# RoPE on 16 heads: the first tile's store cut into its first row and its other three rows

## The chip, the core and the metric

The kernel runs on one core of one Trainium2 chip. Its time is the device time of one execution in microseconds, as the median of several runs. One further execution was recorded by the hardware profiler; every duration of an instruction or a transfer below comes from that one.

## What is computed

Rotary position embedding with the heads split out. For x of 16 x 512 x 1024 floats, 16 heads of 64 numbers and tables cos and sin of 512 x 32:

```python
x = x.reshape(batch, seq, num_heads, head_dim)
x1, x2 = x[..., :half_dim], x[..., half_dim:]
rotated = concatenate([x1 * cos - x2 * sin, x1 * sin + x2 * cos], axis=-1)
```

So each number is read once and written once, 33.6 MB each way, with two products and one sum for each.

## The kernel before

**Tiles and rows.** Two batches form a group, so there are eight groups of 1024 positions. A group lies on 128 partitions with eight positions each; one position of every partition is a "row" here, 128 x 1024 floats or 4 KB per partition. There are 64 rows, u = 0 to 63. A tile is what one transfer moves: the first and the last group are cut into two tiles of four rows (2 MB), the six groups between are one tile of eight rows (4 MB). That makes ten tiles, 0 to 9, and rows 0 to 3 are tile 0.

**The ring.** `x_sb` holds 40 rows, five groups. Results are written over the input rows in it, so a load into the ring's second round (tiles 6 to 9) has to wait until the store of the group that lay there has landed.

**A row's work.** POOL multiplies the row, its halves swapped, by the signed sine table into `t2_sb` (line 252; mostly two rows at a time, eight rows of buffer). DVE multiplies the row by the cosine table into PSUM, `t1_ps` (line 286; three rows of buffer). Then either DVE adds the two back into the ring (line 297), or, for three rows in eight from row 4 to row 59, PE adds `t2_sb` to PSUM through an identity matrix (line 216) and ACT copies the result into the ring (line 183). For one row in eight of the large tiles DVE makes the sine product itself (line 279). All engines go through the rows in order, coupled by counting semaphores.

**Who issues transfers.** ACT issues the loads (`load`, line 152): tile 0, the two tables, then tiles 1 to 5 at the start. Each load of the second round stands in ACT's program behind the copy of a given row, and ACT first waits there until all stores of the old group have landed; `sem_out[k]` counts 16 for each store of group k, and `stores_of(k)` says how many there are. Copies of later rows are behind that wait. SP issues the stores (line 160): at the last row of each tile it waits until all sums up to that row are made (`wait_added`), and stores the tile. In the page and the views, q10 is ACT's queue of loads and q1 is SP's queue of stores; both are served by the same 16 DMA engines. A transfer reaches each DMA engine as eight packets, one for each of eight partitions: 16 KB each for a tile of four rows, 32 KB for one of eight.

Of the kernel before, what the change touches and what calls it, by code (L numbers as in the profile page):

```python
# [6 lines left out]
def bass_split_heads_rope_kernel(  # L7
# [20 lines left out]
    P = 128  # L28
    R1 = seq // P
# [11 lines left out]
    tiles = []  # L41
# [35 lines left out]
    with ExitStack() as stack:  # L77
        x_sb = stack.enter_context(nc.sbuf_tensor([P, RING, H, 2, HALF], fp32))
# [9 lines left out]
        sem_out = [stack.enter_context(nc.semaphore(f"out{k}")) for k in range(EARLY)]  # L88
# [20 lines left out]
        outr = out.rearrange("(c b) (s r) h d -> c (b s) r (h d)", b=2, r=R2)  # L109
        xs = x_sb[:].rearrange("p n h t d -> p n (h t d)")  # L110

        def in_dram(view, t):
            c, r0, n = tiles[t]
            return view[c][:, r0:r0 + n, :].rearrange("p r d -> p (r d)")

        def in_sbuf(t):
            c, r0, n = tiles[t]
            k = (c * R2 + r0) % RING
            return x_sb[:, k:k + n].rearrange("p n h t d -> p (n h t d)")

        def where(u):
            t, r = rows[u]
            return t, r, u % RING
# [7 lines left out]
        def wait_added(eng, u):  # L131

            if n_pe[u]:
                eng.wait_ge(sem_a, n_pe[u])
            if n_comb[u]:
                eng.wait_ge(sem_v, n_comb[u])
# [9 lines left out]

        def stores_of(k):

            return sum(c == k for c, _, _ in tiles)

        def load(eng, t):
            eng.dma_start(in_sbuf(t), in_dram(xr, t)).then_inc(sem_in[t], 16)  # L152
# [1 line left out]
        def on_sync(sp):  # L154
            for u in range(NU):
                t, r, k = where(u)
                if r == tiles[t][2] - 1:
                    wait_added(sp, u)
                    k = u // R2
                    sp.dma_start(in_dram(outr, t), in_sbuf(t)).then_inc(sem_out[k] if k < EARLY else sem_rest, 16)  # L160
            sp.wait_ge(sem_rest, 16 * sum(stores_of(k) for k in range(EARLY, NU // R2)))

        def on_scalar(ae):
            later = {}
            for t, (c, r0, n) in enumerate(tiles):
                if c * R2 + r0 + n <= RING:
                    load(ae, t)
                else:

                    later.setdefault((c * R2 + r0 - RING) // R2 * R2 + R2 - 1 + LAG, []).append(t)  # L170
                if t == 0:
                    for i, (table, sem) in enumerate(((cos, sem_cos), (sin, sem_sin))):
                        ae.dma_start(stage[:, i, :], table.rearrange("(s r) d -> s (r d)", r=R1)).then_inc(sem, 16)  # L173

            ae.wait_ge(sem_i, 2)
            ae.activation(pick[:], ident[:].rearrange("q (s h) -> q h s", h=2)[:, :, None, :].broadcast_to([P, 2, 2, P // 2]), COPY).then_inc(sem_g, 1)  # L176
            ae.wait_ge(sem_t, 2)
            ae.activation(s_sb[:, :, 0, :].rearrange("p (h r) d -> p h r d", h=2), tab_ps[:, :, 1], COPY, scale=-1.0)  # L178
            ae.activation(s_sb[:, :, 1, :].rearrange("p (h r) d -> p h r d", h=2), tab_ps[:, :, 1], COPY).then_inc(sem_s, 1)  # L179
            for u in range(NU):  # L180
                if PE2[u]:
                    ae.wait_ge(sem_e, n_pe[u])
                    ae.activation(xs[:, u % RING, :], t1_ps[:, u % NT1, :], COPY).then_inc(sem_a, 1)  # L183
                for t in later.get(u, ()):
                    k = tiles[t][0] - RING // R2
                    ae.wait_ge(sem_out[k], 16 * stores_of(k))
                    load(ae, t)
# [71 lines left out]
        def on_vector(ve):  # L259
# [44 lines left out]
            for u in range(NU + LEAD):  # L304
                if u < NU:
                    mul(u)
                if u >= LEAD and not PE2[u - LEAD]:
                    comb(u - LEAD)

        on_sync(nc.sync)  # L310
        on_scalar(nc.scalar)
        on_gpsimd(nc.gpsimd)
# [35 lines left out]
```

## Time and profile before

| | |
|---|---|
| median of 3 runs | 161.16 us (161.14 to 161.43) |
| the profiled execution | 161.35 us, span 159.9 us |
| busy: DVE, POOL, PE, ACT | 129.3, 131.8, 66.7, 23.7 us |
| DMA | 67.25 MB, mean 420 GB/s |
| stores: issue at (us) | 22.30, 33.67, 49.99, 65.83, 82.88, 102.95, 119.22, 135.56, 144.50, 150.83 |
| from issue to landing (us) | 19.3, 22.6, 25.6, 29.3, 29.8, 24.4, 21.3, 14.6, 10.6, 9.1 |
| second-round loads: issue at (us) | 56.31, 75.61, 95.16, 95.53 |
| from issue to landing (us) | 33.3, 33.4, 28.4, 42.6 |

The span runs from the first to the last instruction. In the page's row of slices each digit is the busy share of one fortieth of the span, in tenths. In the rows of the timeline the first number is the start, the second how long it lasted, then engine, line, operation and tiles; what stands in brackets is the idle time of that engine ahead of it and what ended it. ACTq and SPq are instructions that only issue a transfer. A DMA share over 1.00 comes from counting a packet whole in the stretch in which it starts.

### The profile page before, as it was taken

How to read it: one execution, taken by the hardware profiler on the slowest of the kernel's cores; microseconds unless marked ns; L12 is line 12 of the kernel's file. 1: busy time of each engine (PE TensorE's matmuls, PEld its weight loads, DVE VectorE, ACT ScalarE, POOL GpSimd, SP SyncE). 2: the span in 40 equal slices, each digit the busy share in tenths (PEclk: the TensorE clock that was granted, in tenths of full speed). 3: DMA queues.
4: the chain of work that ended last, by engine and by line, in shares of the span. 5: the costliest groups of instructions: out<-in, count | busy, mean ns of one | idle time of the engine just before them, and what ended most of it. 6: DMA issues, size and time to landing. Idle time of an engine off the chain costs nothing.

```text
span 159.9 us, 494 instructions
## 1 busy us (share of the span) xinstructions
PE 66.7 (42%) x94; PEld 22.6 (14%) x94; DVE 129.3 (81%) x115; ACT 23.7 (15%) x25; POOL 131.8 (82%) x41
## 2 busy tenths in 40 slices
PE   6050006338932762286209540098509860880000
PEld 1020002012301220122002110022102220220000
DVE  0009986799999999999799927999999989989700
ACT  0410000202220222020400204002500250031000
POOL 1009999999999999999999999599999999598000
PEclk9999999999995799569965998555985589567555
DMA  5999998999999999999999999999999999999896
GB/s 164 411 441 459 393 508 344 447 406 426 471 406 447 479 393 395 492 418 402 418 492 393 418 492 402 402 475 389 479 397 418 451 418 488 410 402 484 373 438 279
DMA packets 3169, 67.25 MB, mean 420 GB/s; under 512 B 352, under 2 KB 608, under 8 KB 608
## 3 DMA queue, kind: packets, MB, share of 16 engines
q10 hardware_dynamic: 1728, 33.69, 49.8%
q1 hardware_dynamic: 1440, 33.56, 48.7%
q14 instruction: 1, 0.01, 0.0%
HBM read 33.69 MB, written 33.55 MB: 420 GB/s over the span
## 4 chain that ended last, share of the span: by engine, by line
DMA 49%; DVE 16%; POOL 13%; issue 7%; PE 6%; ACT 2%; ACTq 1%; DVEq 0%; SPq 0%
DMA x_sb<-in_x_dram 27%; DMA out_dram<-x_sb 18%; POOL t_sb L252 13%; DVE x_sb L297 8%; DVE t_ps L286 6%; PE t_ps L216 5%; DMA stage<-in_sin_dram 4%; DVE t_sb L279 2%; ACT x_sb L183 1%; PE tab_ps L200 1%; ACTq L152 0%; ACTq L173 0%; ACT s_sb L178 0%; ACT s_sb L179 0%; DVE tab_ps L265 0%
## 5 line engine op out<-in xcount | busy, mean ns | idle before, releaser
L252 POOL TENSOR_TENSOR t_sb<-x_sb,s_sb 128x2048 f32<-128x2048 f32 (+1 forms) x35 | 131.1, 3775 | 14.9 <-ACT s_sb L179 10.3
L216 PE MATMUL t_ps<-t_sb,ident 128*128 128x512 f32 x84 | 61.9, 888 | 70.6 <-DVE t_ps L286 48.8
L286 DVE TENSOR_TENSOR t_ps<-x_sb,tab_ps 128x1024 f32<-128x1024 f32 x64 | 76.7, 1221 | 17.4 <-ACT s_sb L179 10.5
L297 DVE TENSOR_TENSOR x_sb<-t_ps,t_sb 128x1024 f32<-128x1024 f32 x43 | 52.3, 1219 | 3.2 <-POOL t_sb L252 3.1
L183 ACT ACTIVATE x_sb<-t_ps 128x1024 f32<-128x1024 f32 x21 | 21.3, 1024 | 111.6 <-PE t_ps L216 100.2
L216 PEld LDWEIGHTS t_ps<-t_sb,ident 128*128 128x128 f32 x84 | 20.7, 273 | 111.4 <-DVE t_ps L286 78.8
L279 DVE TENSOR_TENSOR t_sb<-x_sb,tab_ps 128x1024 f32<-128x1024 f32 x6 | 7.3, 1215 | 0.0
L200 PE MATMUL tab_ps<-stage,pick 128*128 128x256 f32 x4 | 2.0, 667 | 4.8 <-DMA stage<-in_sin_dram 4.8
L193 PE MATMUL t_ps<-zero 128*128 128x512 bf16 x6 | 2.7, 630 | 1.3 <-DVE zero L260 1.3
L200 PEld LDWEIGHTS tab_ps<-stage,pick 128*128 128x128 f32 x4 | 1.2, 324 | 5.9 <-issue 5.7
L176 ACT ACT_TABLE_LOAD x1 | 1.3, 1283 | 4.8 <-issue 4.8
L193 PEld LDWEIGHTS t_ps<-zero 128*128 128x128 bf16 x6 | 0.7, 138 | 2.3 <-DVE zero L260 1.2
L178 ACT ACTIVATE s_sb<-tab_ps 128x256 f32<-128x256 f32 x1 | 0.4, 384 | 4.4 <-PE tab_ps L200 4.4
L260 DVE MEMSET zero<- 128x256 uint32 x1 | 0.3, 272 | 0.9 <-PEq L330 0.9
L227 POOL MEMSET ident<- 128x128 f32 x1 | 0.2, 205 | 0.3 <-POOLq L330 0.3
L176 ACT ACTIVATE pick<-ident 128x256 f32<-128x256 f32 x1 | 0.4, 430 | 0.0
L179 ACT ACTIVATE s_sb<-tab_ps 128x256 f32<-128x256 f32 x1 | 0.4, 378 | 0.0
L229 POOL TENSOR_SCALAR_AFFINE_SELECT ident<-ident 128x128 f32<-128x128 f32 x1 | 0.3, 294 | 0.1
L330 POOL MEMSET const-float32-0.0<- 128x1 f32 x1 | 0.1, 99 | 0.3 <-issue 0.3
L265 DVE TENSOR_SCALAR tab_ps<-tab_ps 128x32 f32<-128x32 f32 x1 | 0.2, 189 | 0.0
L330 POOL MEMSET const-bfloat16-1.0<- 128x1 bf16 x1 | 0.1, 102 | 0.0
L330 POOL MEMSET const-uint8-127<- 128x1 uint8 x1 | 0.1, 102 | 0.0
(1 smaller groups left out, 0.1 us busy)
## 6 DMA issues: line engine op xcount, KB each, us to landing
x_sb<-in_x_dram ACTq DMA_DIRECT2D x6, 4096.0 KB, 33.5
out_dram<-x_sb SPq DMA_DIRECT2D x6, 4096.0 KB, 25.0
x_sb<-in_x_dram ACTq DMA_DIRECT2D x4, 2048.0 KB, 19.9
out_dram<-x_sb SPq DMA_DIRECT2D x4, 2048.0 KB, 14.9
stage<-in_cos_dram ACTq DMA_DIRECT2D x1, 64.0 KB, 7.3
stage<-in_sin_dram ACTq DMA_DIRECT2D x1, 64.0 KB, 7.0
```

Of the source, the lines that this page charges most:

```text
L176: ae.activation(pick[:], ident[:].rearrange("q (s h) -> q h s", h=2)[:, :, None, :].broadcast_to([P, 2, 2, P // 2]), COPY).then_inc(sem_g, 1)
L178: ae.activation(s_sb[:, :, 0, :].rearrange("p (h r) d -> p h r d", h=2), tab_ps[:, :, 1], COPY, scale=-1.0)
L179: ae.activation(s_sb[:, :, 1, :].rearrange("p (h r) d -> p h r d", h=2), tab_ps[:, :, 1], COPY).then_inc(sem_s, 1)
L183: ae.activation(xs[:, u % RING, :], t1_ps[:, u % NT1, :], COPY).then_inc(sem_a, 1)
L193: pe.matmul(t1_ps[:, k, b * BANK:(b + 1) * BANK], zero[:, 0:P], zero[:], start=True, stop=True).then_inc(sem_w, 1)
L200: pe.matmul(tab_ps[:, h].rearrange("p c r d -> p (c r d)"), pick[:, h].rearrange("q b s -> q (b s)"), stage[:].rearrange("q c f -> q (c f) ...
L216: ins = pe.matmul(t1_ps[:, u % NT1, b * BANK:(b + 1) * BANK], ident[:], t2[:, b * BANK:(b + 1) * BANK], start=False, stop=True, skip_group ...
L252: pl.tensor_tensor(t2_sb[:, u % NT2:u % NT2 + n], x_sb[:, k:k + n, :, ::-1, :], table[:, :, None, :, :].broadcast_to([P, n, H, 2, HALF]), ...
L279: ve.tensor_tensor(t2_sb[:, u % NT2, :, :, :], swapped(k), over_heads(tab_ps[:, 0, 1, V_ROW - 1:V_ROW + 1, :]), mult)
L286: ve.tensor_tensor(t1_ps[:, u % NT1, :].rearrange("p (h d) -> p h d", d=HALF), x_sb[:, k, :, :, :].rearrange("p h t d -> p (h t) d"), tab_ ...
L297: ve.tensor_tensor(xs[:, k, :], t1_ps[:, u % NT1, :], t2_sb[:, u % NT2, :, :, :].rearrange("p h t d -> p (h t d)"), add,).then_inc(sem_v, 1)
L330: nc = _bacc.Bacc("TRN2", target_bir_lowering=False, num_devices=1)
```

## The change

SP stores tile 0 in two transfers. As soon as row 0 is added it issues the store of that row alone, 128 x 4 KB; after row 3, where the whole tile was stored, it issues rows 1 to 3, 128 x 12 KB. Both count on `sem_out[0]`, which therefore gets three increments of 16 for group 0 where it got two. The other nine tiles are stored as they were.

```diff
         def stores_of(k):
-            return sum(c == k for c, _, _ in tiles)
+            return sum(c == k for c, _, _ in tiles) + (k == 0)
+
+        def rows_dram(p0, p1, r0, r1):
+            return outr[0][p0:p1, r0:r1, :].rearrange("p r d -> p (r d)")
+
+        def rows_sbuf(p0, p1, r0, r1):
+            return x_sb[p0:p1, r0:r1].rearrange("p n h t d -> p (n h t d)")
...
         def on_sync(sp):
             for u in range(NU):
                 t, r, k = where(u)
-                if r == tiles[t][2] - 1:
+                if u == 0:
+                    wait_added(sp, u)
+                    sp.dma_start(rows_dram(0, P, 0, 1), rows_sbuf(0, P, 0, 1)).then_inc(sem_out[0], 16)
+                elif u == R1 - 1:
+                    wait_added(sp, u)
+                    sp.dma_start(rows_dram(0, P, 1, R1), rows_sbuf(0, P, 1, R1)).then_inc(sem_out[0], 16)
+                elif r == tiles[t][2] - 1:
```

## The prediction

> **What bounds the kernel now.** I read the page's slices and queues first, then the stretches of the DMA queues, then the order of time around the waits. The page:
>
> ```profile
> DMA  5999998999999999999999999999999999999896
> ...
> DMA packets 3169, 67.25 MB, mean 420 GB/s; under 512 B 352, under 2 KB 608, under 8 KB 608
> ...
> q10 hardware_dynamic: 1728, 33.69, 49.8%
> q1 hardware_dynamic: 1440, 33.56, 48.7%
> ```
>
> The 16 DMA engines are busy from slice 2 to slice 38 of 40. Queue q10 (loads, issued by ACT) and q1 (stores, issued by SP) take 49.8 + 48.7 = 98.5% of the span, 157.6 of 159.9 us. The rest is the start (no packet before 1.8 us) and the end of the last store. The view of stretches agrees; its columns end with the granted clock, DMA share and GB/s:
>
> ```profile
> 56.00:138.00 82.00, 39.24 (x58) 13.25 (x57) 76.00 (x68) 14.12 (x14) 77.59 (x20) 0.76 1.00 429
> 138.00:150.00 12.00, 5.41 (x7) 1.53 (x6) 11.52 (x11) 2.05 (x2) 9.15 (x3) 0.64 0.99 429
> 150.00:154.00 4.00, 0.00 (x0) 0.00 (x0) 0.76 (x1) 0.00 (x0) 0.00 (x0) 0.50 1.02 438
> ```
>
> DMA is the bound. DVE and POOL (the third and fifth figures) are close behind and finish at 150.8, just ahead of the last stores. So the question is not whether a store can start earlier, but whether the same bytes cost more, and whether the DMA engines run dry anywhere.
>
> How the two queues share an engine, from the DMA view of four stretches (150 to 153, 57 to 67, 27 to 35 us); columns are packets, MB, share of 16 engines:
>
> ```profile
> q1 hardware_dynamic: 79, 1.29, 100.6%
> ```
> ```profile
> q10 hardware_dynamic: 70, 2.29, 53.1%
> q1 hardware_dynamic: 67, 2.20, 51.0%
> ```
> ```profile
> q10 hardware_dynamic: 71, 2.33, 70.8%
> q1 hardware_dynamic: 64, 1.05, 30.6%
> ```
>
> A 16 KB packet takes 1.006 x 3 x 16 / 79 = 0.611 us, a 32 KB load packet 0.531 x 10 x 16 / 70 = 1.214 us. So a packet costs (1.214 - 0.611) / 16 = 0.0377 us per KB and 0.008 us fixed. In the third stretch tile 0's 16 KB stores lie beside 32 KB loads: the counts are nearly equal (71 and 64), the time is not (70.8 and 30.6%). The queues take turns packet by packet, and the queue with small packets gets the smaller share.
>
> **The change part by part.** Nothing moves on DVE, POOL, PE or ACT; SP issues 11 stores for 10. The sum is made against the profiled execution, 161.35 us (its span 159.9 and 1.45 around it), 0.19 above the median 161.16.
>
> *Cost of the bytes.* Each DMA engine had eight 16 KB packets for tile 0 and gets eight of 4 KB (0.008 + 0.151 = 0.159) and eight of 12 KB (0.460): 8 x (0.159 + 0.460 - 0.611) = 0.06 us. Each transfer also leaves one small packet per engine (352 under 512 B are 22 transfers x 16); one more costs the fixed 0.008. Together **+0.07 us**. The extra SP issue (0.33 us) lies in SP's idle time: SP waited 21.5 us for the fourth sum.
>
> *When tile 0 and what follows is stored.* The first sum ends at 14.12 + 1.23 = 15.35, and SP issues 0.03 later, as it does for the fourth (22.27, issue at 22.30). That issue's first packet came 3.9 us on (none up to 26.2, 11 by 27.0), so row 0 starts at 19.3. Before: eight turns of 1.214 + 0.611, and one in which the store only closes: 15.8 us from 26.2 is 42.0; less 1.2 for the turn that a load gives up as tile 3's load closes in that time: 40.8 (on record 22.30 + 19.3 = 41.6). After: row 0, 8 x (1.214 + 0.159) + 1.2 = 12.2; rows 1 to 3, 8 x (1.214 + 0.460) + 1.2 = 14.6; 19.3 + 26.8 = 46.1, less 2.4 for two loads that close (tiles 2 and 3): 43.7. Tile 0 starts 6.9 us earlier and lands **2.9 us later**, since 17 turns beside big loads replace 8. If all of row 0 went in one turn, it would be done before 26.2 and tile 0 land 8 x 0.151 = 1.2 us earlier; equal counts in 2-us stretches (16 and 16 at 59 to 61) speak for turns of one packet. I take +2.9.
>
> *Who waits for that.* Tiles 1, 2 and 3 were issued (33.67, 49.99, 65.83) before the store ahead had landed, so they land 2.9 later too, at some 59, 78 and 98 us. ACT waits for these landings before it issues loads into the ring, and its PSUM copies are queued behind:
>
> ```profile
> 75.61 0.33 ACTq L152 DMA_DIRECT2D x_sb<-in_x_dram  x1
> 76.00 1.94 ACT L183 ACTIVATE x_sb<-t_ps 128x1024 f32<-128x1024 f32 x2 [4.21 <-DMA out_dram<-x_sb]
> ```
> ```profile
> 95.16 0.86 ACTq L152 DMA_DIRECT2D x_sb<-in_x_dram  x2
> 96.06 1.94 ACT L183 ACTIVATE x_sb<-t_ps 128x1024 f32<-128x1024 f32 x2 [7.23 <-DMA out_dram<-x_sb]
> ```
> ```profile
> 97.12 2.36 DVE L286 TENSOR_TENSOR t_ps<-x_sb,tab_ps 128x1024 f32<-128x1024 f32 x2 [4.14 <-ACT x_sb L183]
> ```
>
> DVE lost 1.12 us at 77.05 and 4.14 at 97.12 to this. With landings 2.9 later it resumes at 80.0 and 100.0: 2.9 in all, as the first delay moves the second wait's start along. From 97.2 to 150.8 DVE is busy 52.33 of 53.60, so at most 1.3 is made up. The last store is issued at 150.83 + 1.6 to 2.9 = 152.4 to 153.7.
>
> *Whether that reaches the end.* The store ahead of it lands at 144.50 + 10.6 = 155.1, and the last one at 150.83 + 9.1 = 159.9; its own data take 8 x 0.611 = 4.9, so landing follows the data by 0.3 to 0.4, and its first packet went at 154.7. With no load beside it an issue needs 1.0 us to its first packet (the kernel's first: 0.80 to 1.8); beside loads 3.9. The tail has no loads: 1.0. So 153.4 to 154.7 meets 154.7: cover is used up, nothing is lost. The store issued at 135.56 becomes 138.5 and needs its turn when the one ahead ends, at 119.22 + 21.3 - 0.4 = 140.1: enough. Loads, served more while stores have small packets, land 2 to 3 us earlier, which removes POOL's wait for the last load (1.94 at 138.16). Loads not yet due: tile 2 lands at 23.3, in the row's first turns some 0.5 later, and POOL needs it at 29.9.
>
> Sum: 161.35 + 0.07 = 161.42; on the median **161.25** (161.16 + 0.07, rounded up).
>
> A rule of the Trainium skill speaks against the change: "DMA: Bandwidth & Descriptors", section "Rules for kernel authors", wants at least 1 MiB per transfer for full bandwidth, and the page's anatomy section gives some 2.0 us fixed per DMA; the row's 0.5 MiB would by that, as an estimate, add up to 2 us if nothing covered it. Here a store follows a store with the DMA share at 1.02 (150 to 154 us), so the trace shows no such gap between queued transfers.
>
> **The rivals.** (1) *Later landings reach the end, slower.* One mechanism: tile 0's small packets, ACT's ring wait, DVE, last store. It decides once the last store's first packet comes after 154.7. With landings 4.1 later (no turn saved by loads that close) and nothing made up, the issue is at 154.9, the packet at 155.9: +1.2; with 3.9 us to the first packet and the 2.9 above, 152.4 + 3.9 = 156.3 to 157.6: +1.6 to +2.9. I price it at +0.8, 162.0, from 161.6 to 163. For it: DVE has no slack after 97. Against: no loads at the end. (2) *Stretched loads, slower.* Beside tile 0's store a load packet took 0.708 x 8 x 16 / 71 = 1.276 us and not 1.214. Some 8 load packets per engine lay there, 8 x 0.062 = 0.5 us; now 16 do: +0.5, 161.7. Against: nothing shows that it depends on the store. (3) *Faster.* The reverse of that stretch, or landings 1.2 earlier. Earlier landings alone shorten DVE's waits but not the DMA work, so they give nothing; a stretch that is gone gives -0.5, 160.75. (4) *A transfer's fixed time stands open* once: +2, 163.2; the gapless stores speak against it. That the change fails to start row 0 early is out: SP had nothing else to wait for.
>
> **How the numbers follow.** Forecast, DMA bound and cover just enough: 0.47 (161.0 to 161.5). Rival 1: 0.24. Rival 2: 0.09. Rival 3: 0.18. Rival 4: 0.02. A measurement tells about 0.2% from no change, 0.32 us. Faster 0.18, within 0.47, slower 0.35. The range 160.8 to 162.3 leaves out the upper part of rival 1, rival 4 and the lower half of rival 3, some 0.18.
>
> **What would show it.** Right: tile 0's two stores land near 31 to 32 and 44 us; ACT's load issues come near 59, 78.5 and 98; DVE's two waits grow to nearly 3 us more in all; POOL's wait on the last load is gone; DMA share stays at 1.0 up to 158. Wrong: those landings come no later (turns are not by packet), load packets beside tile 0 differ from 1.276, or a gap of DMA share before the last store.

## The result and the profile after

| | before | changed |
|---|---|---|
| median | 161.24 us (18 runs, 161.14 to 161.97) | 161.85 us (18 runs, 161.32 to 162.35) |
| profiled execution | 161.35, span 159.9 | 162.29, span 160.9 |
| last store: issue, from issue to landing | 150.83, 9.1 | 151.70, 9.1 |

The changed kernel takes 1.0029 times as long (95% interval 1.0016 to 1.0042): slower by 0.6 us at the median, a little over the 0.2% that the prediction took as not told from no change. Its runs also spread wide: the fastest (161.32) is next to the median of before, the slowest 1.1 us above it.

The page of the changed kernel, the lines that answer to those of before:

```profile
DMA  5999999999999999999999999999999999999994
...
DMA packets 3314, 67.25 MB, mean 418 GB/s; under 512 B 369, under 2 KB 625, under 8 KB 753
...
q10 hardware_dynamic: 1728, 33.69, 49.4%
q1 hardware_dynamic: 1584, 33.56, 48.5%
```

The shares give 97.9% of 160.9 = 157.5 us of DMA work for the mean DMA engine; before it was 98.5% of 159.9 = 157.5. **The mean work has not changed.** What has changed is how evenly the 16 DMA engines end. Every transfer leaves one packet under 512 B on each DMA engine as it closes (23 transfers x 16 are 368 of the 369 above), so the DMA view of short stretches counts closings. Near the end, in the stretches 158.4 to 159, 159 to 159.6 and from 159.6 on, before:

```profile
DMA packets 16, 0.05 MB, mean 82 GB/s; under 512 B 13, under 2 KB 13, under 8 KB 13
```
```profile
DMA packets 3, 0.00 MB, mean 0 GB/s; under 512 B 3, under 2 KB 3, under 8 KB 3
```
```profile
DMA packets 0, 0.00 MB, mean 0 GB/s; under 512 B 0, under 2 KB 0, under 8 KB 0
```

and in the changed kernel:

```profile
DMA packets 16, 0.03 MB, mean 55 GB/s; under 512 B 14, under 2 KB 14, under 8 KB 14
```
```profile
DMA packets 2, 0.02 MB, mean 27 GB/s; under 512 B 1, under 2 KB 1, under 8 KB 1
```
```profile
DMA packets 2, 0.02 MB, mean 5 GB/s; under 512 B 1, under 2 KB 1, under 8 KB 1
```

Before, 13 of 16 are done by 159 us and the last by 159.6. After, 14 are done by 159, and one DMA engine still has data to move after 159.6; it closes some 0.35 us before the landing at 151.70 + 9.1 = 160.8. That one sets the time. In all 14 profiled executions of this study the time is the close of the last DMA engine plus 1.76 to 1.92 us: before, it closes at 159.58 and the time is 161.35; after, 160.52 and 162.29. The other 15 close at much the same times in both, from 158.56 to 159.23 before and from 158.48 to 159.26 after.

The chain of waits by engine points elsewhere. Before, then after:

```profile
DMA 49%; DVE 16%; POOL 13%; issue 7%; PE 6%; ACT 2%; ACTq 1%; DVEq 0%; SPq 0%
```
```profile
DVE 35%; DMA 24%; issue 13%; PE 9%; POOL 9%; ACT 3%; ACTq 1%; DVEq 0%; SPq 0%
```

By that the kernel has turned from DMA bound to DVE bound, and the waits that feed this chain did grow. The changed kernel's timeline:

```profile
77.82 1.94 ACT L195 ACTIVATE x_sb<-t_ps 128x1024 f32<-128x1024 f32 x2 [6.20 <-DMA out_dram<-x_sb]
```
```profile
78.88 1.23 DVE L298 TENSOR_TENSOR t_ps<-x_sb,tab_ps 128x1024 f32<-128x1024 f32 x1 [3.11 <-ACT x_sb L195]
```
```profile
98.77 2.36 DVE L298 TENSOR_TENSOR t_ps<-x_sb,tab_ps 128x1024 f32<-128x1024 f32 x2 [3.97 <-ACT x_sb L195]
```

DVE resumes at 78.88 and 98.77 where it was 77.05 and 97.12. So two theories stood against each other:

- **Theory T, the tail:** later landings delay ACT and DVE, and the last store comes too late (the prediction's rival 1).
- **Theory S, the slowest DMA engine:** the chain of stores has cover, and the kernel ends when the slowest of 16 DMA engines has done its share; the change makes that one later.

### The profile page after: what moved, and what is told of

Its sections match the earlier page's. It is cut to its first block, busy times and chain, and to the rows that moved or that the text cites. A ratio compares the mean times of both kernels' runs of the same rounds, so it can differ in the third digit from the quotient of the medians.

```text
span 160.9 us, 495 instructions
## 1 busy us (share of the span) xinstructions
PE 65.7 (41%) x94; PEld 22.5 (14%) x94; DVE 129.2 (80%) x115; ACT 23.7 (15%) x25; POOL 131.7 (82%) x41
## 3 DMA queue, kind: packets, MB, share of 16 engines
q10 hardware_dynamic: 1728, 33.69, 49.4%
## 4 chain that ended last, share of the span: by engine, by line
DVE 35%; DMA 24%; issue 13%; PE 9%; POOL 9%; ACT 3%; ACTq 1%; DVEq 0%; SPq 0%
DMA out_dram<-x_sb 19%; DVE x_sb L309 16%; DVE t_ps L298 16%; POOL t_sb L264 9%; PE t_ps L228 8%; DMA stage<-in_sin_dram 4%; DVE t_sb L291 3%; ACT x_sb L195 3%; PE tab_ps L212 1%; ACTq L158 1%; ACTq L185 0%; ACT s_sb L190 0%; ACT s_sb L191 0%; DVE tab_ps L277 0%; DVEq L308 0%
## 5 line engine op out<-in xcount | busy, mean ns | idle before, releaser
L228 PE MATMUL t_ps<-t_sb,ident 128*128 128x512 f32 x84 | 60.9, 874 | 71.6 <-DVE t_ps L298 57.0
## 6 DMA issues: line engine op xcount, KB each, us to landing
out_dram<-x_sb SPq DMA_DIRECT2D x1, 1536.0 KB, 20.8
```

The costliest lines, as they stand in the source:

```text
L228: ins = pe.matmul(t1_ps[:, u % NT1, b * BANK:(b + 1) * BANK], ident[:], t2[:, b * BANK:(b + 1) * BANK], start=False, stop=True, skip_group ...
```

## The experiments

Each was timed beside the kernel before on the same chip; ratios are to it, with 95% intervals.

**1. The changed kernel again**, for a second trace.

> The changed kernel once more, for a second trace. Theory S (one straggling DMA engine): the mean DMA engine closes the last store at 158.8 us of the span as before, but one of the 16 closes 1 to 2 us behind the rest and sets the end; time 161.6 to 162.1. Theory T (the tail: tile 0's store lands later, ACT's wait for it delays DVE, and the last store comes too late): most DMA engines show a gap ahead of the last store and all close some 0.5 us later than before; time 161.6 to 162.1.

Measured: 161.80 us, 1.0026 (1.0013 to 1.0040). The profiled execution of this run took 161.31 us, as little as the kernel before, with its last store issued at 152.75, 1.05 us *later* than in the trace that took 162.29. Its closings in the three stretches are 10, 6 and 0; the last two of these:

```profile
DMA packets 6, 0.00 MB, mean 0 GB/s; under 512 B 6, under 2 KB 6, under 8 KB 6
```
```profile
DMA packets 0, 0.00 MB, mean 0 GB/s; under 512 B 0, under 2 KB 0, under 8 KB 0
```

The same program, a later last store and a faster run: against T. That the slowest DMA engine closes 1 us earlier (159.54 for 160.52), and so nearer to the rest, is S.

**2 and 3. ACT's waits taken off the copies**, in the changed kernel and in the one before:

```diff
-    LAG = 10
+    LAG = 14
```

> The changed kernel with ACT's second-round loads placed four rows later in its program (LAG 14 for 10), so that ACT no longer waits for landings ahead of its copies, and DVE's waits of 3.1 and 4.0 us go. The last store is then issued at some 147 to 149 us, not 151.7. Theory T: the cost of the change is gone, 161.2 to 161.35 us. Theory S: the last store's issue does not matter, 161.6 to 162.0 us.

> The kernel before with LAG 14. DVE's waits of 1.1 and 4.1 us go, the last store is issued at 147 to 148 us. Both theories have the DMA engines busy to the end, so 161.15 to 161.35, as before. Were it faster by over 0.3 us, the kernel before would have been bound by the tail, which neither theory says.

Measured: the changed kernel with it 161.59 us, 1.0020 (1.0002 to 1.0037); the kernel before with it 161.44, 1.0012 (1.0003 to 1.0021). Waits and SP's last issue in the former:

```profile
DVE t_ps L298 <- ACT x_sb L195: 0.8, 2, 0.4
```
```profile
147.34 0.33 SPq L172 DMA_DIRECT2D out_dram<-x_sb  x1
```

DVE's waits for ACT fell from 7.9 us to 0.8 and the last store is issued 4.4 us earlier, yet most of the cost may still be there; its runs reach from 161.21 to 162.36, as wide as the changed kernel's. T's forecast failed. The median lies at the lower edge of S's, and the intervals of 1 and 2 overlap, so whether a small part went is not told. The kernel before got slower by 0.1% from losing its DVE waits (1.6 us left of 6.9), which neither theory said.

**4. The split without the early start:** both transfers after row 3.

```diff
-                if u == 0:
-                    wait_added(sp, u)
-                    sp.dma_start(rows_dram(0, P, 0, 1), ...)
+                if u == 0:
+                    continue
                 elif u == R1 - 1:
                     wait_added(sp, u)
+                    sp.dma_start(rows_dram(0, P, 0, 1), ...)
                     sp.dma_start(rows_dram(0, P, 1, R1), ...)
```

> The two transfers, both issued after row 3: the split without the early start. Tile 0's turns start at 26.2, not 18.6, so tile 0 lands 6.5 to 7.5 us later than in the changed kernel (49 to 50 us), tile 1 at 63 to 65, and ACT's first wait for landings lasts until then. Theory T: DVE loses 6 to 8 us more, the last store is issued at 156 to 159 us, and the time is 164 to 167 us. Theory S: the same chain, but it costs only what passes the cover of 2 to 3 us: 162.5 to 165 us. If the time stayed at 161.9, the landings would not matter at all.

Measured: 162.15 us, 1.0052 (1.0036 to 1.0068), less than either theory gave. ACT's first load of the second round went at 62.85 (57.41 in the changed kernel), its third at 99.04 (96.78): of 5.4 us of delay 2.3 are left. While the load queue is dry, the stores have the DMA engines to themselves and catch up. The last store is issued at 154.63, and here the tail does show: all 16 DMA engines close late, between 160.38 and 160.55. DMA share (last figure but one) in 154 to 156 us:

```profile
154.00:156.00 2.00, 0.00 (x0) 0.00 (x0) 0.56 (x1) 0.00 (x0) 0.00 (x0) 0.50 0.71 303
```

**5. Each row of tile 0 alone.** SP issues a store after each of rows 0 to 3, four transfers of 4 KB packets.

```diff
-                if u == 0:
+                if u < R1:
                     wait_added(sp, u)
-                    sp.dma_start(rows_dram(0, P, 0, 1), ...)
+                    sp.dma_start(rows_dram(0, P, u, u + 1), ...)
```

> Each row of tile 0 stored alone as it is added: four transfers of 4 KB packets. 36 turns for 18 in the changed kernel, so tile 0 lands some 15 us later (57 to 60 us) and group 0 at 71 to 75; ACT waits for it from 58 on, the load queue runs dry for some 5 to 10 us, in which the store queue has the DMA engines alone. Both theories: DVE loses 10 us or more, the last store is issued past 160 us, and the time is 168 to 175 us. If turns are not by packet, the landing hardly moves and the time stays below 162.5.

Measured: 161.65 us, 1.0020 (1.0009 to 1.0030): far off my forecast. Group 0 landed at 33.43 + 29.6 = 63.0, not 71 to 75, for the reason of experiment 4: the loads ran dry after 57 us, and tile 1's store then met no load packets. The last store was issued at 153.56 and landed 6.3 us later, with no store left ahead of it. In this execution, which took 161.31 us, all 16 DMA engines closed between 159 and 159.6:

```profile
DMA packets 16, 0.00 MB, mean 0 GB/s; under 512 B 16, under 2 KB 16, under 8 KB 16
```

This gives the tail's bound: issue plus 6.3. A tail that ends at 159.9, as the kernel before did, may have its last issue at 153.6. The changed kernel's 151.70 left 1.9 us of cover.

**6. Three rows, then one.**

```diff
-                if u == 0:
-                    sp.dma_start(rows_dram(0, P, 0, 1), ...)
+                if u == R1 - 2:
+                    sp.dma_start(rows_dram(0, P, 0, R1 - 1), ...)
                 elif u == R1 - 1:
-                    sp.dma_start(rows_dram(0, P, 1, R1), ...)
+                    sp.dma_start(rows_dram(0, P, R1 - 1, R1), ...)
```

> Rows 0 to 2 stored after row 2, row 3 after row 3: the same two sizes as in the changed kernel in the other order, started 2.3 us before the kernel before and 4.6 us after the changed one. By turns tile 0 lands 4 to 5 us later than in the changed kernel (46 to 47 us), group 0 at 60 to 62. Theory T: last store issued at 153 to 155 us, time 162.2 to 164. Theory S: cover of 2 to 3 us holds for most of it, 161.6 to 162.6.

Measured: 161.46 us, 1.0016 (0.9993 to 1.0038), not told from no change, and below both forecasts. Its profiled execution was the slowest of the study but one, 163.19 us, with the last store issued at 153.35. In the stretches 159 to 159.6 and from 159.6 on:

```profile
DMA packets 16, 0.02 MB, mean 27 GB/s; under 512 B 15, under 2 KB 15, under 8 KB 15
```
```profile
DMA packets 3, 0.03 MB, mean 10 GB/s; under 512 B 1, under 2 KB 1, under 8 KB 1
```

Fifteen DMA engines are done where a fast run ends; one is 2 us behind. That is S; by T all 16 would be late.

**7. Two halves by partitions**, both after row 3, with 16 KB packets as before.

```diff
+                if u == R1 - 1:
+                    sp.dma_start(rows_dram(0, P // 2, 0, R1), ...)
+                    sp.dma_start(rows_dram(P // 2, P, 0, R1), ...)
```

> Tile 0 stored after row 3 in two transfers of 64 partitions each, 16 KB packets as before: one transfer more, no small packets, no early start. Tile 0 lands one turn (1.2 us) later than in the kernel before, much as in the changed kernel. Theory S (the slowest of 16 DMA engines ends the kernel; the change makes that one later): if one more transfer is what does it, 161.6 to 161.9 us; if the small packets or the early start do, 161.2 to 161.35. Theory T (late tail): as the changed kernel, 161.7 to 161.9.

Measured: 161.56 us, 1.0013 (1.0001 to 1.0024): between the forecast for "one more transfer does it" and the one for "it does not", so it settles neither.

**8 and 9. As many transfers as before, and one fewer.** Row 0 early and rows 1 to 7 in one transfer; then rows 0 to 7 in one.

```diff
+                elif u == R2 - 1:
+                    sp.dma_start(rows_dram(0, P, 1, R2), ...)    # in 9: 0, R2, and no row 0 ahead
```

> Row 0 stored early as in the changed kernel, then rows 1 to 7 in one transfer after row 7: as many transfers as the kernel before (10), with the early 4 KB packets. Group 0 lands at about 57 us (37.5 us to the first packet, then 8 turns of 1.214 + 1.06 and one that closes), so the chain through ACT and DVE is as in the changed kernel. If the eleventh transfer is what costs, the time is 161.2 to 161.35 us; if the early small packets cost, 161.6 to 161.9. Late tail: not decided by it, the last store still has some 1 us of cover.

> Group 0 stored once, rows 0 to 7 after row 7: nine transfers, no small packets, and the first store 11 us later than before. Group 0 lands at 56 to 58 us. If each transfer costs by itself, 160.9 to 161.2 us, under the kernel before; if the slowest DMA engine's one fetch of instructions sets the floor, 161.2 to 161.4. Only a dry DMA queue could make it slower, and the loads alone fill the DMA engines until 37 us.

Measured: 161.44 us, 1.0010 (0.9997 to 1.0024), and 161.44, 1.0010 (0.9997 to 1.0022). Neither is told from no change. The first median lies between the values that I had set for "the eleventh transfer" and "the small packets"; the second lies above both of its forecasts. So they settle nothing, but for one thing: a gain per transfer saved is not there.

**10 and 11. Load one DMA engine, change nothing else.** The kernel before with waits on SP that are already met; they become 128 and 320 instructions ahead of the first store (the pages count 622 and 814 for 494). SP is through with them in time: its first store goes at 22.26 and 22.15, for 22.30.

```diff
         def on_sync(sp):
+            for _ in range(256):      # 640 in 11
+                sp.wait_ge(sem_z, 1)
```

> The kernel before with 256 waits that are already met ahead of SP's first store: SP is idle then, so only its instructions have to be fetched (some 16 KB more, by the DMA engines). Theory S: the fetches take turns on one DMA engine and delay it by some 0.66 us each (in the kernel before a fetch record of 309 ns is followed by a store packet 350 ns longer than the others), so the slowest engine ends 0.6 to 1.3 us later if it is that engine: 161.8 to 162.6. Theory T: nothing waits for SP, so the time is 161.2 to 161.35 us.

> The kernel before with 640 idle waits on SP (320 instructions, some 19 us, done before the first store at 22.3), for 256 (128 instructions), which added one fetch record and 0.44 us. Slowest DMA engine: two or three fetches, 0.4 us each on the same DMA engine, 162.0 to 162.6 us, and the last DMA engine closes 1.3 to 1.9 us behind the mean. If the fetches spread over DMA engines: 161.8 again. If fetches were not the cause: 161.3.

Measured: 161.79 us, 1.0026 (1.0014 to 1.0038), its fastest run at 161.53, at the lower edge of S's forecast; and 163.69, 1.0145 (1.0126 to 1.0165), above the highest forecast, 162.6. Queue q14, which fetches instructions, in the kernel before, in 10 and in 11:

```profile
q14 instruction: 1, 0.01, 0.0%
```
```profile
q14 instruction: 2, 0.02, 0.0%
```
```profile
q14 instruction: 4, 0.03, 0.0%
```

The kernel before has one fetch in its span, at 63.1 us: one record of 0.31 us on one DMA engine, and the store packet behind it takes 1.57 us for 1.214, together 0.66 us. (The changed kernel also has one, at 60.6; its page counts a second record on q14, of 40 bytes.) One more raised the time by 0.44 us (161.79 less 161.35 beside it), three more by 2.4 (163.69 less 161.32). A load of 8 KB on one of 16 DMA engines, in 67 MB, costs nearly as much as the change: this shows S for the kernel before. In 11 the stretches 159 to 159.6 and from 159.6 on show it:

```profile
DMA packets 16, 0.02 MB, mean 27 GB/s; under 512 B 15, under 2 KB 15, under 8 KB 15
```
```profile
DMA packets 4, 0.05 MB, mean 14 GB/s; under 512 B 1, under 2 KB 1, under 8 KB 1
```

Fifteen DMA engines close by 159.35, one at 161.98. That one also delivers the last load late (POOL waits 6.0 us for loads, 1.9 before), which takes the tail along: the last issue is at 153.37.

Which DMA engine a packet ran on is not recorded, but it can be worked out. Without a gap, a packet's record starts 3 or 4 ns before the end of the one ahead of it on its DMA engine (all 1761 steps after 60 us in the changed kernel can be put so), and every DMA engine gets the same packets of each transfer; so the records fall into 16 lanes, one for each DMA engine. In the kernel before the lane with the fetch closes last, at 159.58. The added fetch does not join it. In 10 it comes at 9.8 us and its lane closes last, at 159.97; the fetch at 60.5 lies in another lane, which closes at 159.34. So a fetch counts only as far as its DMA engine ends behind the others, and 0.66 us on another one cost 0.44. In 11 at least two of the three added fetches lie in the lane that closes at 161.98; the fetch at 60.6 lies in one that closes at 159.35.

**12. Both at once:** the 256 waits in the changed kernel.

> The changed kernel with the same 256 idle waits on SP that added 0.44 us to the kernel before. They add one fetch of instructions to the DMA engine that fetches already. If the changed kernel's loss sits on that same DMA engine, the two add up: 162.1 to 162.4 us, and one DMA engine closes some 1.0 to 2.2 us behind the mean of 158.9. If its loss sits on other DMA engines or in the chain of stores, the later of the two counts alone: 161.75 to 161.95 us.

Measured: 161.64 us, 1.0019 (1.0002 to 1.0037): below both forecasts, of which the interval reaches only the one for the later of the two alone. The two do not add up, and the forecast for "the same DMA engine" rested on a premise that does not hold in the profiled execution: the two fetches lie in two lanes. The lane of the added fetch (9.6 us) closes at 159.67. The lane of the other (60.7 us) closes last, at 159.94, and has a store packet of 1.60 us at 126.2 besides.

## Why the prediction was right or wrong

The time fell into the range, but the likeliest case did not come true: 161.25 was forecast within 0.2%, 161.85 came, slower. That the range held is luck: rivals 1 and 2, priced at 162.0 and 161.7, had stretched it upward, and the time came out near their prices by neither's mechanism.

- **Cost of the bytes: right.** The DMA view of the changed kernel in 20 to 28 us, where row 0 is stored beside loads:

```profile
q10 hardware_dynamic: 112, 3.15, 91.1%
q1 hardware_dynamic: 111, 0.45, 13.8%
```

  A 4 KB packet takes 0.138 x 8 x 16 / 111 = 0.159 us, as worked out. Counts are equal again: a turn is one packet, of 4 KB too. The Trainium skill, "DMA: Bandwidth & Descriptors", section "Queues, rings and completion order", has a DMA engine drain a whole packet of some 9 to 17 descriptors before it switches; by that row 0's eight would go in one turn. Here row 0 needed 14.0 us from issue to landing, and the measurement decides.
- **The landings: right direction, too large.** ACT's load issues came 1.1, 1.8 and 1.6 us later (57.41, 77.44, 96.78), for 2.9. Row 0 was issued at 15.21, and tile 0 landed at 22.14 + 20.8 = 42.9 for 41.6, 1.3 later. Row 0 landed at 29.2, not at 31 to 32: its first packet came 3.4 us after the issue, not 3.9, and from there it took 10.6 us, not 12.2.
- **DVE's waits: right in kind, too large.** 3.11 + 3.97 and 0.4 at 59.84, 2.2 us more than before for "nearly 3"; DVE resumed 1.1 and 1.2 us ahead of the 80.0 and 100.0 forecast. As forecast, the second wait did not grow. POOL's wait for the last load is gone.
- **The cover of the last store: right.** The DMA share stays at 1.05 and 0.96 in 150 to 154 and 154 to 158; no gap. The issue came at 151.70, ahead of the 152.4 to 153.7 that I gave. So rival 1, later landings that reach the end, did not happen here; it shows in experiment 4, with the last issue at 154.63.
- **Rival 2, stretched loads: wrong.** The loads took 49.4% of 160.9 = 79.5 us of the mean DMA engine, 79.6 before. In the stretch above 96 of the 112 load packets carry data and 16 close, so a load packet beside row 0's stores took 0.911 x 8 x 16 / 96 = 1.215 us. The 1.276 before was a mean of 71 packets, of which 23 took over 1.29 us, in bursts; such bursts come in the changed kernel too (29 of 80 in the same 27 to 35 us), and what causes them is not shown.
- **Rival 4, 2 us for a transfer: wrong.** Three more transfers in experiment 5 cost 0.2%, 0.3 us. The section of the Trainium skill's page that gave 2.0 us is about transfers issued from GpSimd; here ACT and SP issue them.
- **The step that failed** is "DMA is the bound", worked out as "Sum: 161.35 + 0.07". It summed the work of the mean DMA engine. The bound is the slowest one, which already ended 0.66 us behind through its fetch. In the profiled run of the changed kernel three packets took 1.50, 1.40 and 1.78 us (starts 96.4, 120.9, 126.6) for 1.214, 1.03 us in all, and the last close moved by 0.9. Put in lanes, all three lie with the fetch of 60.6 on the DMA engine that closes last; fetch and long packets together cost it 1.83 us after 60 us, while 13 of the other 15 lost nothing.
- **What stays open:** why packets are long, and why the slowest DMA engine is later in most executions of the changed kernel, as their times suggest; only two of these were profiled (last close 160.52 and 159.54). In the executions profiled it is not the tail (1, 2), and it is not more work. Long packets are not the changed kernel's alone (three of 1.28 to 1.45 us at 124.8 to 125.1 in the kernel before), nor the fetching DMA engine's: in experiment 6 the one that closes last, at 161.41, has no fetch and packets of 2.36, 1.59, 1.57 and 1.83 us. The number of transfers, the packet size and the early start are not told apart by 7 to 9, and the intervals of all these variants overlap. No version beat the kernel before.

## What to carry to other kernels

When 16 DMA engines are busy from start to end, ask when the slowest ends and not what the mean has to do: count the closings in the last stretches. Here an earlier store gained nothing, while anything that lands on one DMA engine, even a fetch of instructions, can count as far as that one ends behind the others. A chain of waits that changes from DMA to DVE is a reason to try DVE, not a proof; taking those waits away (experiment 2) cost one line.

## What the runs showed of the hardware that was not expected

- 128 instructions more on an idle sequencer cost 0.26%, 320 cost 1.45%, through the DMA engine that fetches them. It is not the same one for all fetches (experiments 10 to 12). The Trainium skill, "DMA: Bandwidth & Descriptors", section "Queues, rings and completion order", names queue row 14 as the runtime's own; the records on q14 agree, and here that row competes with the kernel's data.
- A late store corrects itself: with the load queue dry, tile 1's store ran alone, and group 0's landing came at 63 us and not at 71 to 75.
- Two executions of one program (experiment 1) differ by 1.0 us, and so do the closings of the last of 16 DMA engines (160.52 and 159.54); the other 15 close by 159.26 and 159.33.
